# Two PSUM accumulators of a weight block: their matmuls alternate instead of following each other

## The chip, the cores and the metric

The kernel runs on one core of a Trainium2 chip. The metric is device time in microseconds, the median of several executions of the whole kernel on that core. A core has a matmul engine (TensorE; PE in the profile, its weight loads PEld), a vector engine (VectorE, DVE), a scalar engine (ScalarE, ACT), GpSimd (POOL) and DMA queues that SyncE (SP) and ScalarE issue here. [...]

## The reference

A decoder trunk of two layers on 256 tokens of width 2048, in fp32. Each layer projects the stream, mixes it, gates it, projects it back and normalizes it:

```python
def reference(x, mem, w_in, w_out, w_mem_kv, ln_g, ln_b, pool_w, pool_scale, w_kv_shared):
    h = x
    split_at = [BRANCH_WIDTH, 2 * BRANCH_WIDTH, 2 * BRANCH_WIDTH + MEM_WIDTH]
    for i in range(DEPTH):
        if i == N_A_LAYERS:
            k_blocks, v_blocks, k_mean = moba_shared_kv(h, w_kv_shared)
        u = h @ w_in[i]
        branch_in, gate_b, mem_q, gate_m = jnp.split(u, split_at, axis=-1)
        if i < N_A_LAYERS:
            branch = multiscale_pool(branch_in, pool_w[i], pool_scale[i])
        else:
            branch = moba_attention(branch_in, k_blocks, v_blocks, k_mean)
        mem_o = memory_attention(mem_q, mem, w_mem_kv[i])
        mixed = jnp.concatenate([branch * jax.nn.silu(gate_b), mem_o * jax.nn.silu(gate_m)], axis=-1)
        y = mixed @ w_out[i]
        h = layer_norm(DEEPNORM_ALPHA * h + y, ln_g[i], ln_b[i])
    return h
```

Layer 0 mixes by trailing means over 2, 4, 8 and 16 tokens and a small matrix per group, layer 1 by causal attention with 12 heads over the 256 tokens (one block, so no block selection is left). Both also attend to 256 memory tokens with 4 heads.

## The kernel before

Products are made exact enough by splitting: each fp32 operand becomes a rounded part (hi) and the exact rest (lo), both of type fp32r, and a product is hi·hi + hi·lo + lo·hi. The activations lie transposed as `xT`, `memT` and `zT` with the hi columns (256 tokens) beside the lo columns (256 tokens), 16 tiles along the contraction (k-tiles).

The weights stream through the kernel as a list of items, each one block of 128 x 1024. `run` (line 118) walks through the list: a block is loaded by SyncE 4 items ahead into one of 4 buffers `raw`, is split 3 items ahead (`LP`) by ScalarE (the rounded copy `wh`, line 68) and VectorE (the rest `wl`, line 69) into one of 4 buffers each, and is then consumed by TensorE. The code is written in the order in which each engine runs it; no scheduler moves anything (`manual_schedule`), and the semaphores between the engines follow from who reads what.

Two functions consume nearly all blocks.

- `proj_t` (line 152) makes 256 output channels, with the weights as the stationary operand. A block holds 4 k-tiles by 256 channels; two accumulators `acc[0]` and `acc[1]`, one PSUM bank each, take 128 channels each. For each k-tile and accumulator there are two matmuls: `wh` against the 512 hi and lo columns of the activations, and `wl` against the 256 hi columns. A block is 16 matmuls, four blocks make a projection. At the last k-tile (k = 15) the 256-column product comes first. There are 42 such projections: 168 blocks.
- `proj_n` (line 178) makes 512 output channels with the activations stationary. A block holds 2 k-tiles by 512 channels; accumulators `acc[0]` and `acc[1]` take 128 tokens each. For each k-tile and accumulator there are three matmuls of 512 columns: hi·`wh`, hi·`wl`, lo·`wh`. A block is 12 matmuls, eight blocks make a projection. There are 12 such projections: 96 blocks.

All blocks run through the matmul call at line 64. Inside a block, all matmuls of `acc[0]` stand before all of `acc[1]`; in the last block of a projection `done(0, acc[0])` stands behind the matmuls of `acc[0]`, `done(1, acc[1])` at the end. `done` is the reader of the accumulator: `fold` (lines 205 and 206: ScalarE copies the lo half, VectorE adds the hi half), or a split into values, or the addition to the residual with its statistics (lines 380 and 381). The accumulators rotate through four banks.

Between blocks stand the pieces of attention (`a`, `b`, `c` of the pairs, planned by `later` a given number of items ahead), the small pooling products (`pool_mix`, 256 columns each) and the transposes. At the end, `last` (line 705) multiplies the last output columns by weights that wait in the buffers of `xT` and `memT`.

Of the kernel before, what the change touches and what calls it, by code (L numbers as in the profile page):

```python
# [17 lines left out]
P = 128  # L18
T = 256                 # tokens (and memory tokens)
D = 2048  # L20
KT = D // P             # contraction tiles of a projection
HD = 128
# [9 lines left out]

BLK = 1024              # columns of a weight block: 4 k-tiles x 256 or 2 k-tiles x 512
RAW_BUFS = 4
W_BUFS = 4
LD = 4                  # blocks that loads run ahead
LEAD = 3                # first blocks, whose parts are read in turns
LD0 = 8                 # blocks that are loaded at once at the start
LP = 3                  # blocks that the splitting runs ahead


@with_exitstack
def trunk(ctx: ExitStack, tc: tile.TileContext, a: dict, out: bass.AP):
# [4 lines left out]

    # operands of products: [hi | lo] per tile, both exact in fp32r
    xT = sb.tile([P, KT, 2 * T], F32R, name="xT")  # L50
# [10 lines left out]

    # ---------------------------------------------------------------- basics
    def mm(o, l, r, start, stop):
        nc.tensor.matmul(o, l, r, start=start, stop=stop)  # L64

    def split(hi, lo, src):
        """hi = src rounded to fp32r, lo = the exact rest."""
        nc.scalar.activation(hi, src, AF.Copy)  # L68
        nc.vector.tensor_sub(lo, src, f(hi))  # L69

    # ---------------------------------------------------------------- stream
    items = []

    def collect(fn, *args):
        """The items that fn adds, taken out of the list."""
        base = len(items)
        fn(*args)
        got = items[base:]
        del items[base:]
        return got  # L80
# [5 lines left out]
    now = [0]  # L86
# [63 lines left out]

    # ---------------------------------------------------------------- projections
    def proj_t(mov, wblk, done):
        """256 output channels on partitions: done(n, psum[128, 512]) for n in 0, 1, where the
        products of hi and of lo tokens lie side by side."""
        acc = []

        def consume(kb):
            def go(wh, wl, k0=0, k1=4):
                if not acc:
                    acc.extend(ps.tile([P, 512], F32, name="acc", bufs=4) for _ in range(2))  # L160
                h = wh.rearrange("p (k n) -> p k n", n=256)
                l = wl.rearrange("p (k n) -> p k n", n=256)
                for n in range(2):
                    s = slice(n * P, (n + 1) * P)
                    for kk in range(k0, k1):
                        k = 4 * kb + kk
                        if k < KT - 1:
                            mm(acc[n], h[:, kk, s], mov[:, k], k == 0, False)
                        mm(acc[n][:, :T], l[:, kk, s], mov[:, k, :T], False, False)
                        if k == KT - 1:  # L170
                            mm(acc[n], h[:, kk, s], mov[:, k], False, True)
                    if kb == 3:
                        done(n, acc[n])
            return go
        for kb in range(4):
            item(wblk[kb], BLK, consume(kb))

    def proj_n(sta, wblk, done, korder=range(8), banks=("acc", "acc")):
        """512 output channels, tokens on partitions: done(t, psum[128, 512]) for t in 0, 1."""
        acc = []  # L180
        korder = list(korder)

        def consume(j, kb):
            def go(wh, wl):
                if j == 0:
                    acc.extend(ps.tile([P, 512], F32, name=b, bufs=4 if b == "acc" else 1) for b in banks)
                h = wh.rearrange("p (k n) -> p k n", n=512)
                l = wl.rearrange("p (k n) -> p k n", n=512)
                for t in range(2):
                    for kk in range(2):  # L190
                        k = 2 * kb + kk
                        xh = sta[:, k, t * P:(t + 1) * P]
                        xl = sta[:, k, T + t * P:T + (t + 1) * P]
                        first, last = j == 0 and kk == 0, j == 7 and kk == 1
                        mm(acc[t], xh, h[:, kk], first, False)
                        mm(acc[t], xh, l[:, kk], False, False)
                        mm(acc[t], xl, h[:, kk], False, last)
                    if j == 7:
                        done(t, acc[t])
            return go  # L200
# [16 lines left out]
    def to_gate(dst, base):  # L217
        """2 silu(x) = x (1 + tanh(x / 2))"""
        def done(n, acc):
# [19 lines left out]

    # ---------------------------------------------------------------- attention  # L240
    class Rows:
        """Row softmax in three steps: statistics, exponentials, division."""

# [20 lines left out]
    def gated(o, g, kt):  # L264
        """zT[kt] = o * silu(gate), of which g is the double"""
        zf = sb.tile([P, T], F32, name="zf", bufs=3)
# [49 lines left out]
    class MobaPair(Rows):  # L316
        """Two heads of causal attention over the own block: rows 0-127 see keys 0-127."""

# [31 lines left out]
        def c(self):  # L350
            v, g = self.st["v"], self.st["g"]
            o = ps.tile([P, 2, T], F32, name="o")
            for j in range(2):
                h = self.h0 + j
                # columns of ph: keys 0-127 of rows 0-255, then keys 128-255 of rows 128-255
                for m, (d, s) in enumerate(((o[:, j], slice(0, T)), (o[:, j, P:], slice(T, 384)))):
# [8 lines left out]
    def plan(pr, a, b, c):  # L365
        """Steps of a pair, by blocks from now: one engine's turn in each."""
        later(a, pr.a)
# [5 lines left out]

    # ---------------------------------------------------------------- residual and norm
    lnst = {}
# [33 lines left out]

    # ---------------------------------------------------------------- constants  # L410
    nc.vector.memset(eps_t[:, 0:1], EPS)
# [18 lines left out]

    # ---------------------------------------------------------------- memory branch
    st = {}

    def fresh(key, make):
        """st[key], as a tile that is allocated when its first part is written."""
        tiles = []
# [26 lines left out]
    def after(fn):  # L463
        """Attach fn to the item last added."""
        it = items[-1]
# [21 lines left out]

    # ================================================================ layer 0
    def load_act(t, src, kb):
        item(a[src][kb], BLK, None, ("act", t, kb))  # L490

    # memory keys and values side by side, while the activations arrive
    k0 = fresh("k", lambda: heads_tile("kk"))
# [17 lines left out]
    def pool_group(g):  # L511
        """Trailing means less the token, of the 384 channels in U, into zT as operands; as steps."""
        u = (U0, U1)[g % 2]
        src, d = u, 1
# [53 lines left out]
    def weave(main, extra):  # L568
        """An extra item after each of the first main ones."""
        for j, it in enumerate(main):  # L570
# [29 lines left out]

    # ================================================================ between the layers
    gbs = {}
# [6 lines left out]
    def h_transpose(kp):  # L609
        """Two k-tiles of the normed stream, transposed."""  # L610
        pt = ps.tile([P, 2, T], F32, name="pt" if kp % 2 else "o")
# [14 lines left out]

    # ================================================================ layer 1
    mem_q_gate(1)
# [18 lines left out]

    # the last columns of the output weights wait in the buffers of xT and memT
    def out_1():
        for n in range(3):  # L650
            proj_n(zT, [a["w_out"][1, n, kb] for kb in range(8)], to_residual(n), KORDER)

    # rows [g, g, g - g_hi, b, b - b_hi], the first of each rounded to fp32r: what the last
    # norm adds, (m0 - mean) / std * g + b, is one product of depth 5 with them
    gbt = {}
# [27 lines left out]

    # ================================================================ program
    items[0]["cuts"] = (0, T, 2 * T, BLK)
# [42 lines left out]

    # the last rows are centred by the mean of their first columns before all are known
    m0 = sb.tile([P, 2], F32, name="m0")  # L730
# [22 lines left out]

    # the last rows: (r - m0) g / std plus the product above, but for the first columns
    mv = sb.tile([P, 2], F32, name="mv", bufs=2)
# [28 lines left out]
def _cols_t(w):  # L784
    """[2048, N] -> [N/256, 4, 128, 4*256]: blocks of four k-tiles by 256 columns."""
    n = w.shape[1] // 256
# [3 lines left out]
def _cols_n(w):  # L790
    """[2048, N] -> [N/512, 8, 128, 2*512]: blocks of two k-tiles by 512 columns."""
    n = w.shape[1] // 512
# [3 lines left out]
def _act_t(x):  # L796
    """[256, 2048] -> [4, 128, 4*256]: transposed, blocks of four k-tiles."""
    return x.T.reshape(4, 4, P, T).transpose(0, 2, 1, 3).reshape(4, P, BLK)
# [37 lines left out]
```

## Time and profile before

| what | value |
|---|---|
| median of 3 runs | 829.24 us (828.7 to 829.42) |
| span of the profiled execution, first to last instruction | 826.7 us |
| own time of the profiled execution | not listed apart; the three runs lie 2.0 to 2.7 us above the span |
| TensorE busy | 813.9 us, 98% of the span |
| VectorE, ScalarE, GpSimd busy | 68%, 48%, 0% |
| matmuls, weight loads | 4436 each |
| mean granted TensorE clock | 0.997 |

How to read it: a row of the timeline is an instruction, or several equal ones in a row (x2), with its start and its duration. Matmuls are pipelined, so the duration of one (0.39 us for 512 columns) is longer than the distance to the start of the next; the distance of starts is what a matmul takes from the engine's time.

### The profile page before, as it was taken

How to read it: one execution, taken by the hardware profiler on the slowest of the kernel's cores; microseconds unless marked ns; L12 is line 12 of the kernel's file. 1: busy time of each engine (PE TensorE's matmuls, PEld its weight loads, DVE VectorE, ACT ScalarE, POOL GpSimd, SP SyncE). 2: the span in 40 equal slices, each digit the busy share in tenths (PEclk: the TensorE clock that was granted, in tenths of full speed). 3: DMA queues.
4: the chain of work that ended last, by engine and by line, in shares of the span. 5: the costliest groups of instructions: out<-in, count | busy, mean ns of one | idle time of the engine just before them, and what ended most of it. 6: DMA issues, size and time to landing. Idle time of an engine off the chain costs nothing.

```text
span 826.7 us, 11533 instructions
## 1 busy us (share of the span) xinstructions
PE 813.9 (98%) x4436; PEld 700.8 (85%) x4436; DVE 559.0 (68%) x793; ACT 397.3 (48%) x578; POOL 0.2 (0%) x4
## 2 busy tenths in 40 slices
PE   7999999999999999999999999999999999999995
PEld 6888888898888888888888888888888888888885
DVE  5686678667856555797667667576765667568746
ACT  6564555544545333545455445354554445545510
POOL 0000000000000000000000000000000000000000
PEclk9999999999999999999999999999999999999998
DMA  8876446457558655676554545546455554647742
GB/s 315 302 249 205 165 153 203 159 182 227 181 197 273 196 190 191 195 238 200 183 176 146 187 164 170 204 150 197 163 179 167 189 179 153 201 135 247 260 126 102
DMA packets 47163, 159.13 MB, mean 193 GB/s; under 512 B 5375, under 2 KB 7167, under 8 KB 46847
## 3 DMA queue, kind: packets, MB, share of 16 engines
q1 hardware_dynamic: 46080, 155.47, 56.9%
q10 hardware_dynamic: 1028, 2.93, 0.9%
q8 instruction: 34, 0.56, 0.3%
q14 instruction: 21, 0.17, 0.1%
HBM read 156.28 MB, written 2.10 MB: 192 GB/s over the span
## 4 chain that ended last, share of the span: by engine, by line
PE 98%; DVE 0%; DMA 0%; ACT 0%; DVEq 0%; issue 0%; SPq 0%
PE acc L64 89%; PE o L64 4%; PE s L64 2%; PE pt L64 2%; PE pt L347 0%; PE pt L297 0%; DMA raw<-in_w_mk 0%; PE o L615 0%; PE pt L615 0%; DVE res L779 0%; DVE res L760 0%; DVEq L832 0%; DVE stats L718 0%; DVE res L717 0%; ACT wh L68 0%
## 5 line engine op out<-in xcount | busy, mean ns | idle before, releaser
L69 DVE TENSOR_TENSOR wl<-raw,wh 128x1024 fp32r<-128x1024 f32 (+3 forms) x274 | 324.7, 1190 | 179.9 <-ACT wh L68 178.6
L64 PE MATMUL acc<-xT,wh 128*128 128x512 f32 x1216 | 422.0, 394 | 0.0
L68 ACT ACTIVATE wh<-raw 128x1024 fp32r<-128x1024 f32 (+3 forms) x274 | 281.4, 1031 | 220.2 <-PE acc L64 162.2
L64 PE MATMUL acc<-xT,wl 128*128 128x256 f32 x1216 | 327.9, 280 | 0.0
L64 PEld LDWEIGHTS acc<-xT,wh 128*128 128x128 f32 x1216 | 223.6, 188 | 43.5
L64 PEld LDWEIGHTS acc<-xT,wl 128*128 128x128 f32 x1216 | 228.5, 188 | 6.5 <-DVE wl L69 0.2
L64 PE MATMUL acc<-wh,zT 128*128 128x512 f32 x448 | 143.1, 397 | 0.0
L64 PEld LDWEIGHTS acc<-wh,zT 128*128 128x128 f32 x448 | 84.1, 188 | 19.9
L64 PE MATMUL acc<-wl,zT 128*128 128x512 f32 x224 | 88.0, 393 | 0.0
L64 PE MATMUL acc<-wh,xT 128*128 128x512 f32 x192 | 61.0, 396 | 0.0
L205 ACT ACTIVATE fold<-acc 128x256 f32<-128x256 f32 x72 | 27.7, 384 | 56.9 <-PE acc L64 55.8
L64 PE MATMUL acc<-memT,wh 128*128 128x512 f32 x128 | 46.8, 408 | 4.3 <-ACT wh L68 4.3
L64 PEld LDWEIGHTS acc<-wl,zT 128*128 128x128 f32 x224 | 42.1, 188 | 10.0
L64 PEld LDWEIGHTS acc<-wh,xT 128*128 128x128 f32 x192 | 36.0, 188 | 8.7
L64 PE MATMUL acc<-wl,xT 128*128 128x512 f32 x96 | 37.6, 392 | 0.0
L64 PE MATMUL acc<-memT,wl 128*128 128x256 f32 x128 | 35.5, 288 | 0.0
L206 DVE TENSOR_TENSOR fold<-acc,fold 128x256 f32<-128x256 f32 x72 | 29.5, 419 | 4.9 <-ACT fold L205 4.9
L64 PEld LDWEIGHTS acc<-memT,wh 128*128 128x128 f32 x128 | 24.7, 196 | 9.2 <-ACT wh L68 4.3
L68 ACT ACTIVATE zT<-zf 128x256 fp32r<-128x256 f32 x32 | 12.9, 415 | 39.7 <-DVE zf L267 35.4
L64 PEld LDWEIGHTS acc<-memT,wl 128*128 128x128 f32 x128 | 25.0, 196 | 1.0 <-DVE wl L69 0.2
L64 PEld LDWEIGHTS acc<-wl,xT 128*128 128x128 f32 x96 | 18.0, 188 | 4.3
L64 PE MATMUL acc<-xT,zT 128*128 128x256 f32 (+1 forms) x96 | 21.5, 318 | 0.0
(132 smaller groups left out, 617.9 us busy)
## 6 DMA issues: line engine op xcount, KB each, us to landing
raw<-in_w_in SPq DMA_DIRECT2D x128, 512.0 KB, 3.5
raw<-in_w_out SPq DMA_DIRECT2D x64, 512.0 KB, 4.3
raw<-in_w_sk SPq DMA_DIRECT2D x24, 512.0 KB, 4.2
raw<-in_w_sv SPq DMA_DIRECT2D x24, 512.0 KB, 3.5
raw<-in_w_mv SPq DMA_DIRECT2D x14, 512.0 KB, 5.4
raw<-in_w_mk SPq DMA_DIRECT2D x12, 512.0 KB, 4.4
raw<-in_xT SPq DMA_DIRECT2D x4, 512.0 KB, 5.2
res<-in_x ACTq DMA_DIRECT2D x2, 1024.0 KB, 5.7
```

The costliest lines, as they stand in the source:

```text
L64: nc.tensor.matmul(o, l, r, start=start, stop=stop)
L68: nc.scalar.activation(hi, src, AF.Copy)
L69: nc.vector.tensor_sub(lo, src, f(hi))
L205: nc.scalar.activation(dst, acc[:, T:], AF.Copy)
L206: nc.vector.tensor_add(dst, acc[:, :T], dst)
```

## The change

The loops inside a block are turned. In `proj_t`, for each k-tile the two `wh` products (of `acc[0]` and `acc[1]`, 512 columns each) now stand side by side, then the two `wl` products (256 columns each); at k = 15 the `wl` pair comes first. In `proj_n`, for each k-tile the three products are each done for `acc[0]` and at once for `acc[1]`. Both calls of `done` now stand behind all matmuls of the last block. The number and shapes of all matmuls and weight loads stay, and so do the order and number of instructions on ScalarE, VectorE, GpSimd and SyncE. Comments and docstrings are removed, too.

```diff
@@ proj_t
-                for n in range(2):
-                    s = slice(n * P, (n + 1) * P)
-                    for kk in range(k0, k1):
-                        k = 4 * kb + kk
-                        if k < KT - 1:
-                            mm(acc[n], h[:, kk, s], mov[:, k], k == 0, False)
-                        mm(acc[n][:, :T], l[:, kk, s], mov[:, k, :T], False, False)
-                        if k == KT - 1:
-                            mm(acc[n], h[:, kk, s], mov[:, k], False, True)
-                    if kb == 3:
+                for kk in range(k0, k1):
+                    k = 4 * kb + kk
+                    hi = [(acc[n], h[:, kk, n * P:(n + 1) * P], mov[:, k]) for n in range(2)]
+                    lo = [(acc[n][:, :T], l[:, kk, n * P:(n + 1) * P], mov[:, k, :T]) for n in range(2)]
+
+                    for o, wt, m in (hi + lo if k < KT - 1 else lo + hi):
+                        mm(o, wt, m, k == 0 and m.shape[-1] == 2 * T, k == KT - 1 and m.shape[-1] == 2 * T)
+                if kb == 3:
+                    for n in range(2):
                         done(n, acc[n])
@@ proj_n
-                for t in range(2):
-                    for kk in range(2):
-                        k = 2 * kb + kk
-                        xh = sta[:, k, t * P:(t + 1) * P]
-                        xl = sta[:, k, T + t * P:T + (t + 1) * P]
-                        first, last = j == 0 and kk == 0, j == 7 and kk == 1
-                        mm(acc[t], xh, h[:, kk], first, False)
-                        mm(acc[t], xh, l[:, kk], False, False)
-                        mm(acc[t], xl, h[:, kk], False, last)
-                    if j == 7:
+                for kk in range(2):
+                    k = 2 * kb + kk
+                    xh = [sta[:, k, t * P:(t + 1) * P] for t in range(2)]
+                    xl = [sta[:, k, T + t * P:T + (t + 1) * P] for t in range(2)]
+                    first, last = j == 0 and kk == 0, j == 7 and kk == 1
+                    for t in range(2):
+                        mm(acc[t], xh[t], h[:, kk], first, False)
+                    for t in range(2):
+                        mm(acc[t], xh[t], l[:, kk], False, False)
+                    for t in range(2):
+                        mm(acc[t], xl[t], h[:, kk], False, last)
+                if j == 7:
+                    for t in range(2):
                         done(t, acc[t])
```

On TensorE, in the last block of a `proj_t` projection of layer 1 (the accumulators are `acc_4253` and `acc_4254`, the block's split weights `wh_4247` and `wl_4248`), the end of one accumulator and the beginning of the other stood so before:

```order
L64 MATMUL acc_4253<-xT_63,wh_4247 128x512
L64 MATMUL acc_4253<-xT_63,wl_4248 128x256
L64 MATMUL acc_4253<-xT_63,wh_4247 128x512
L64 MATMUL acc_4253<-xT_63,wl_4248 128x256 x2
L64 MATMUL acc_4253<-xT_63,wh_4247 128x512
L64 MATMUL acc_4254<-xT_63,wh_4247 128x512
L64 MATMUL acc_4254<-xT_63,wl_4248 128x256
L64 MATMUL acc_4254<-xT_63,wh_4247 128x512
```

The 512- and 256-column products took turns, but for the last k-tile, where two of 256 and two of 512 columns meet. The end of the same block now:

```order
L64 MATMUL acc_4253<-xT_63,wh_4247 128x512
L64 MATMUL acc_4254<-xT_63,wh_4247 128x512
L64 MATMUL acc_4253<-xT_63,wl_4248 128x256
L64 MATMUL acc_4254<-xT_63,wl_4248 128x256
L64 MATMUL acc_4253<-xT_63,wl_4248 128x256
L64 MATMUL acc_4254<-xT_63,wl_4248 128x256
L64 MATMUL acc_4253<-xT_63,wh_4247 128x512
L64 MATMUL acc_4254<-xT_63,wh_4247 128x512
```

The banks take turns at every matmul, and the sizes now come in pairs: two of 512, two of 256; at the last k-tile four of 256 and then four of 512 with the next projection's first two.

In a `proj_n` block of the output projection of layer 1 (accumulators `acc_6654` and `acc_6655`), the first accumulator's part before was:

```order
L64 MATMUL acc_6654<-wh_6722,zT_65 128x512
L64 MATMUL acc_6654<-wl_6723,zT_65 128x512
L64 MATMUL acc_6654<-wh_6722,zT_65 128x512 x2
L64 MATMUL acc_6654<-wl_6723,zT_65 128x512
L64 MATMUL acc_6654<-wh_6722,zT_65 128x512
L64 MATMUL acc_6655<-wh_6722,zT_65 128x512
```

And now:

```order
L64 MATMUL acc_6654<-wh_6722,zT_65 128x512
L64 MATMUL acc_6655<-wh_6722,zT_65 128x512
L64 MATMUL acc_6654<-wl_6723,zT_65 128x512
L64 MATMUL acc_6655<-wl_6723,zT_65 128x512
L64 MATMUL acc_6654<-wh_6722,zT_65 128x512
L64 MATMUL acc_6655<-wh_6722,zT_65 128x512
```

All have 512 columns before and after; what moves is the bank, and that the same activations are no longer stationary twice in a row.

## Rows read from the trace of the kernel before

**Rows 1.** The page: busy time by engine, and the granted clock in 40 slices.

```profile
PE 813.9 (98%) x4436; PEld 700.8 (85%) x4436; DVE 559.0 (68%) x793; ACT 397.3 (48%) x578; POOL 0.2 (0%) x4
...
PEclk9999999999999999999999999999999999999998
```

**Rows 2.** The page, groups by line: busy us, mean ns | idle before.

```profile
L64 PE MATMUL acc<-xT,wh 128*128 128x512 f32 x1216 | 422.0, 394 | 0.0
...
L205 ACT ACTIVATE fold<-acc 128x256 f32<-128x256 f32 x72 | 27.7, 384 | 56.9 <-PE acc L64 55.8
```

**Rows 3.** Timeline of TensorE, an inner `proj_t` block: start us, duration us.

```profile
464.23 0.39 PE L64 MATMUL acc<-xT,wh 128*128 128x512 f32 x1
...
465.50 0.28 PE L64 MATMUL acc<-xT,wl 128*128 128x256 f32 x1
465.62 0.39 PE L64 MATMUL acc<-xT,wh 128*128 128x512 f32 x1
465.85 0.28 PE L64 MATMUL acc<-xT,wl 128*128 128x256 f32 x1
```

**Rows 4.** Timeline of TensorE: block starts among four `proj_t` projections of layer 0.

```profile
125.63 0.40 PE L64 MATMUL acc<-xT,wh 128*128 128x512 f32 x1
...
128.41 0.39 PE L64 MATMUL acc<-xT,wh 128*128 128x512 f32 x1
...
133.96 0.39 PE L64 MATMUL acc<-xT,wh 128*128 128x512 f32 x1
...
139.53 0.39 PE L64 MATMUL acc<-xT,wh 128*128 128x512 f32 x1
...
145.07 0.39 PE L64 MATMUL acc<-xT,wh 128*128 128x512 f32 x1
...
170.08 0.40 PE L64 MATMUL acc<-xT,wh 128*128 128x512 f32 x1
```

**Rows 5.** Timeline of TensorE: the end of a `proj_t` projection, the next one's beginning.

```profile
471.87 0.39 PE L64 MATMUL acc<-xT,wh 128*128 128x512 f32 x1
472.09 0.40 PE L64 MATMUL acc<-xT,wl 128*128 128x256 f32 x2
472.33 0.63 PE L64 MATMUL acc<-xT,wh 128*128 128x512 f32 x2
472.80 0.28 PE L64 MATMUL acc<-xT,wl 128*128 128x256 f32 x1
```

**Rows 6.** Timeline of TensorE: the first of 18 pooling products, and what follows them.

```profile
172.87 0.40 PE L64 MATMUL pt<-zT,wh 128*128 128x256 f32 x2
...
174.98 0.39 PE L64 MATMUL acc<-xT,wh 128*128 128x512 f32 x1
```

**Rows 7.** Timeline of TensorE, `proj_n`: two rows with 12 matmuls from start to start.

```profile
743.69 0.63 PE L64 MATMUL acc<-wh,zT 128*128 128x512 f32 x2
...
746.49 0.63 PE L64 MATMUL acc<-wh,zT 128*128 128x512 f32 x2
```

**Rows 8.** Timeline of TensorE, in `last`: two rows with 3 matmuls from start to start.

```profile
797.31 0.39 PE L64 MATMUL acc<-memT,zT 128*128 128x512 f32 x1
...
797.99 0.39 PE L64 MATMUL acc<-memT,zT 128*128 128x512 f32 x1
```

**Rows 9.** Timeline of TensorE: the first and the third matmul of the kernel.

```profile
4.28 0.79 PE L64 MATMUL acc<-memT,wh 128*128 128x512 f32 x1 [4.28 <-ACT wh L68]
...
5.12 0.63 PE L64 MATMUL acc<-memT,wh 128*128 128x512 f32 x1
```

**Rows 10.** Timelines of ScalarE, VectorE and TensorE around 54 us.

```profile
51.43 0.60 ACT L68 ACTIVATE vv<-o 128x512 fp32r<-128x512 f32 x1 [0.80 <-PE o L64]
...
53.00 1.22 DVE L69 TENSOR_TENSOR wl<-raw,wh 128x1024 fp32r<-128x1024 f32 x1 [0.26 <-ACT wh L68]
...
54.01 0.40 PE L64 MATMUL acc<-xT,wh 128*128 128x512 f32 x1
54.28 0.39 PE L64 MATMUL acc<-xT,wl 128*128 128x256 f32 x1
```

## The prediction

> **What bounds the kernel now.** I read the page's busy times first, then the groups by line, then TensorE's timeline. TensorE is busy for 813.9 of 826.7 us, at the full granted clock in all slices but the last [rows 1], and the largest group of matmuls has no idle time before it [rows 2]. The other engines are at 68% and less. So the time is the sum of what the 4436 matmuls take one behind the other. A change that only reorders them can act in three ways: it changes the distance from one matmul's start to the next one's, it moves a wait onto TensorE, or it takes one away. The timeline gives the distances. In an inner block of `proj_t`, 512 and 256 columns alternate with 0.23 and 0.12 us, and the eight matmuls of the first accumulator take 1.39 us (464.23 to 465.62) [rows 3]. In `proj_n`, 12 matmuls of 512 columns take 2.80 us, 0.2333 each [rows 7].
>
> **Does a bank that changes make a matmul cheaper?** The trace of before already has such changes, one in the middle of every block and one at its end. At 465.50 the last matmul of one bank starts and at 465.62 the first of the other; the distance, 0.12, and the next, 0.23, are those of the pairs before [rows 3]. Over all of the trace's starts, the 193 changes of this kind (a 256-column product on `xT`, then a 512-column one on another bank) have a mean distance of 118.0 ns, and the 912 that stay in the bank 117.4. I therefore cost the new bank at 0. Both ends: the reading of one row is good to 0.01 us, the two means differ by +0.6 ns; with 1 ns either way and 3840 matmuls (168 blocks of 16, 96 of 12) the term lies between -3.8 and +3.8 us. From 0.43 ns per matmul on it would decide by itself.
>
> **Does the new order of sizes cost something?** This is the term that moves the sum. In `proj_t` the change does more than alternate banks: 512, 256, 512, 256 becomes 512, 512, 256, 256. Before, equal sizes meet only at k = 15, once per accumulator. Four projections of layer 0 run from 125.63 to 170.08 without anything between them, 44.45 us for 16 blocks. Their inner blocks take 5.55 us a pair (128.41 to 133.96) or 5.54 (139.53 to 145.07), 2.7725 each [rows 4]; 16 of these would be 44.36. The other 0.09 us belong to the eight places where two of 256 and two of 512 meet: about 10 ns a place. Rows 5 show one: two of 256 from 472.09 to 472.33, two of 512 from 472.33 to 472.80, 0.71 us, where two alternating pairs take 2.7725/4 = 0.693.
>
> What a place costs when every four matmuls are one is not in the trace, so I bound it. The low end: only the two neighbours of equal size cost what they cost in streams of one size, 0.2333 [rows 7] and, for 18 pooling products of 256 columns, 2.11/18 = 0.1172 [rows 6]; the other two distances stay those of the alternation. Two equal neighbours then take 0.3505 where a pair takes 0.3466, so +4 ns per four. If all four cost what the streams do, it is 2 x 4 = +8 ns. The isolated place, 10 ns, is the high end, with up to 17 by the single row pair above (0.710 - 0.693). I take +8: it lies beside the row with the same operands and tiles (10), and part of those 10 may be the price of falling out of step and back, which a regular pattern doesn't pay each time. There are 42 projections x 16 k-tiles = 672 fours: 672 x 8 ns = +5.4 us. The 84 places that exist already (42 x 2) are dissolved into them: 84 x 10 ns = -0.8 us. `proj_n` has 512 columns before and after, and its distances are the same whether the stationary activations repeat or not as far as a whole block shows it (2.80 us for blocks in which a third of the steps repeat them) [rows 7]: 0, with +-0.5 us for 1152 matmuls at 0.4 ns.
>
> [...]
>
> **What moves on the other engines.** Their instruction order is unchanged, but `done(0)` waits for the end of the block instead of its middle, 1.39 us later [rows 3]. Queued behind the waiting `fold` on ScalarE (0.384 us [rows 2]) is the split of the weight block four items ahead. That costs nothing where the splitting is three blocks ahead, 3 x 2.77 = 8.3 us; without this cover each of the 54 projections could lose that 0.384 us, 21 us in all, but a shift that is absorbed once is not paid again.
>
> The cover is thin at one place. Around 54 us the values' second split on ScalarE starts at 51.43 and takes 0.60; behind it comes the rounding of the next weight block, whose rest VectorE makes from 53.00 to 54.22, and TensorE's second matmul there starts 0.27 behind its first instead of 0.23, the next pair is late as well; the block loses 0.16 us [rows 10]. In the new kernel both splits stand behind the end of the block, so the chain moves by about 0.5 us, while the `wl` operand is wanted 0.23 us later, behind two products of 512. I take +0.2 us (between -0.16 and +0.5).
>
> At the start the opposite happens. The first matmul of the kernel shows 0.79 us, the third, of the same shape, 0.63 [rows 9]: the 0.16 us between them are the second one's wait for `wl`, which VectorE hasn't finished. With two 512-column products in front, `wl` is wanted later by a whole one of them, and the wait goes: -0.2 us (between -0.25 and 0). The two cancel.
>
> **Sum.** 5.4 - 0.8 + 0 = +4.6 us. The span of the profiled execution becomes 826.7 + 4.6 = 831.3; the median of the runs is 2.5 us above that span, and that difference stays: 833.8 us, 0.55% slower.
>
> **Rivals.**
> 1. No change: the fours settle into a step of their own that costs what the alternation costs, or at most the 4 ns of the low end. For it: a matmul of 512 columns takes 0.22 us at one place (471.87 to 472.09) and 0.235 at the next [rows 5]; such distances compensate each other in part, and the average is what counts. Against it: 84 places that all cost something. At 0 ns per four it gives -0.8, 828.4 us; at 4 ns, 2.7 - 0.8 = +1.9, 831.1 us. [...]
> 2. Faster: streams of equal size can run quicker than the alternation. In `last`, 3 matmuls of 512 columns take 0.68 us, 0.2267 each [rows 8], and with 0.1172 for 256 columns a pair would be 0.3439 instead of 0.3466; two pairs in each of 672 fours give -3.6, with the 84 places -4.4 us: 824.8 us. The same sign has a bank turnaround that shows only when every matmul changes its bank: 1 ns is 3.8 us. Against the first: there the moving operand is `xT` or `memT` and the weights are `zT`; where `wh` is stationary and `xT` moves, 512 behind 512 takes 0.235 [rows 5]. With the 84 places gone it decides from 1.2 ns per four on. Against the second are rows 3.
> 3. Much slower: the late `done(0)` makes TensorE wait in each projection. It would take 0.2 us per projection, 54 of them, 11 us: 840 us. Against it stands the cover of three blocks; it would have to eat 8.3 us first.
>
> **How the numbers follow.** A kernel like this tells 0.2% (1.66 us) from no change. The forecast (6 to 14 ns per four, +3.2 to +8.6 us) has 0.58; rival 1 (0 to 6 ns) 0.27, of which 0.03 lie above 3.7 ns, where the bound of 0.2% is crossed; rival 2 0.11, rival 3 0.04. Slower than 830.9: 0.58 + 0.04 + 0.03 = 0.65. Within 0.2%: 0.24. Faster than 827.6: 0.11. The range runs from the lower bound of no change, 827.6, to 12 ns per four with the small terms at their high ends (8.1 - 0.8 + 0.5 = 7.8): 837.0. Outside are rival 2, rival 3 and the top of the forecast, some 0.18. The forecast's own range is 832.4 to 837.8.
>
> **What would show it.** In the new timeline an inner `proj_t` block takes 4 x 8 = 32 ns more than 2.77 us, 2.80 to 2.81; the first and last blocks no longer differ from it much; two of 512 columns take about 0.465 and two of 256 about 0.235. `proj_n` blocks stay at 2.80. TensorE's list of waits has nothing new of over 0.5 us. The prediction is wrong if inner `proj_t` blocks stay at 2.77 or fall below, if `proj_n` blocks leave 2.80 (then the bank or the repeated stationary operand matters), or if waits of TensorE on ScalarE or VectorE appear at ends of projections.

## The result, and the profile after

The kernel after takes 835.18 us (median of 4 runs, 834.62 to 835.64), the kernel before in the same comparison 828.97 us (4 runs, 828.63 to 829.42). The ratio is 1.0074, with a 95% interval of 1.0059 to 1.0088: 0.7% slower. The forecast was 833.8 us. The profiled execution of after has a span of 833.3 us and an own time of 835.62.

From the page of after, the span, the busy times and the largest group of matmuls:

```profile
span 833.3 us, 11533 instructions
...
PE 820.1 (98%) x4436; PEld 702.9 (84%) x4436; DVE 560.6 (67%) x793; ACT 392.6 (47%) x578; POOL 0.2 (0%) x4
...
L64 PE MATMUL acc<-xT,wh 128*128 128x512 f32 x1216 | 379.9, 397 | 0.0
```

Beside [rows 1, 2]: TensorE's busy time grew from 813.9 to 820.1 us with the same 4436 matmuls, nearly the whole 6.6 us of the span, and the large group still has no idle time before it (0.0, the last number of its row). So matmuls became dearer; TensorE did not begin to wait. Its list of waits says the same (engine, line and tile waited for, total us, times, longest):

```profile
PE acc L64 <- ACT wh L68: 4.7, 1, 4.7
PE pt L769 <- DVE cc L766: 2.8, 1, 2.8
PE acc L64 <- ACT cct L771: 0.4, 1, 0.4
```

These three places wait in before too, with 4.3, 2.8 and 0.4 us. The first is the arrival of the first weight block. Five experiments below begin with the same two matmuls as after (banks only, the two with runs of eight, and after with 32 and with 1696 bytes more) and show 4.2 to 4.4 there, so I don't put these 0.4 us down to the change.

Next, TensorE's timeline (start, duration, operation, count): an inner block of `proj_t` in layer 0, from its first two matmuls to those of the next block.

```profile
130.04 0.63 PE L64 MATMUL acc<-xT,wh 128*128 128x512 f32 x2
130.51 0.40 PE L64 MATMUL acc<-xT,wl 128*128 128x256 f32 x2
130.75 0.63 PE L64 MATMUL acc<-xT,wh 128*128 128x512 f32 x2
131.22 0.40 PE L64 MATMUL acc<-xT,wl 128*128 128x256 f32 x2
...
132.87 0.39 PE L64 MATMUL acc<-xT,wh 128*128 128x512 f32 x1
```

The block takes 2.83 us where [rows 4] had 2.7725. A four (two of 512, two of 256) takes 0.71. Over the trace inner blocks come in two lengths, 2.813 and 2.827 us, which is 10.0 and 13.5 ns more per four than before. The distances between neighbours in the inner blocks tell which matmul pays: a 256 that follows a 512 begins 235.5 ns behind it, against 229.2 in the alternation, and a 512 that follows a 512 begins after 232.4, while a matmul behind a 256 begins after 117.4 to 119.1 ns, against 117.5. It is mostly the 512-column products that got dearer, the second of a pair most.

In `proj_n` (here in layer 1) six matmuls take 1.40 us:

```profile
776.27 0.63 PE L64 MATMUL acc<-wl,zT 128*128 128x512 f32 x2
776.74 1.09 PE L64 MATMUL acc<-wh,zT 128*128 128x512 f32 x4
777.67 0.63 PE L64 MATMUL acc<-wl,zT 128*128 128x512 f32 x2
```

That is 0.2333 each, as in [rows 7]. Summed over all distances of starts, `proj_t` on `xT` went from 424.6 to 430.2 us, `proj_t` on `memT` from 47.0 to 47.5, `proj_n` on `zT` from 157.1 to 157.1. With the 0.4 us of the first wait, these are 6.5 of the 6.6 us.

### The profile page after: what moved, and what is told of

It is laid out like the page before. It is cut to its first block, busy times and chain, and to the rows that moved or that the text cites. A ratio compares the mean times of both kernels' runs of the same rounds, so it can differ in the third digit from the quotient of the medians.

```text
span 833.3 us, 11533 instructions
## 1 busy us (share of the span) xinstructions
PE 820.1 (98%) x4436; PEld 702.9 (84%) x4436; DVE 560.6 (67%) x793; ACT 392.6 (47%) x578; POOL 0.2 (0%) x4
## 4 chain that ended last, share of the span: by engine, by line
PE 98%; DVE 0%; DMA 0%; ACT 0%; DVEq 0%; issue 0%; SPq 0%
PE acc L64 89%; PE o L64 3%; PE s L64 2%; PE pt L64 2%; PE pt L349 0%; PE pt L299 0%; DMA raw<-in_w_mk 0%; PE o L617 0%; PE pt L617 0%; DVE res L781 0%; DVE res L762 0%; DVEq L834 0%; DVE stats L720 0%; DVE res L719 0%; ACT wh L68 0%
## 5 line engine op out<-in xcount | busy, mean ns | idle before, releaser
L64 PE MATMUL acc<-xT,wh 128*128 128x512 f32 x1216 | 379.9, 397 | 0.0
L64 PEld LDWEIGHTS acc<-xT,wl 128*128 128x128 f32 x1216 | 223.0, 188 | 52.0 <-DVE wl L69 0.5
L64 PE MATMUL acc<-xT,wl 128*128 128x256 f32 x1216 | 237.0, 281 | 0.0
L64 PEld LDWEIGHTS acc<-xT,wh 128*128 128x128 f32 x1216 | 189.0, 189 | 2.9
L64 PE MATMUL acc<-wh,zT 128*128 128x512 f32 x448 | 124.3, 395 | 0.0
L64 PE MATMUL acc<-wl,zT 128*128 128x512 f32 x224 | 70.6, 396 | 0.0
L64 PE MATMUL acc<-wh,xT 128*128 128x512 f32 x192 | 52.9, 394 | 0.0
L64 PEld LDWEIGHTS acc<-wl,zT 128*128 128x128 f32 x224 | 42.0, 188 | 10.1
L64 PE MATMUL acc<-memT,wh 128*128 128x512 f32 x128 | 41.9, 412 | 4.7 <-ACT wh L68 4.7
L64 PE MATMUL acc<-wl,xT 128*128 128x512 f32 x96 | 30.3, 396 | 0.0
L64 PE MATMUL acc<-memT,wl 128*128 128x256 f32 x128 | 25.6, 287 | 0.0
```

## The experiments

Each is a few lines on the kernel before or after and was timed beside the kernel before on the same chip. The first three take the change apart.

**Banks only.** In `proj_t` the sizes keep alternating, and the bank changes at every second matmul (0, 1, 1, 0), where before changes it twice in a block of 16; both `done` stand at the end.

```diff
+                for kk in range(k0, k1):
+                    k = 4 * kb + kk
+                    for fn, n in (((hi, 0), (hi, 1), (lo, 0), (lo, 1)) if k == 0 else
+                                  ((lo, 0), (hi, 0), (lo, 1), (hi, 1)) if k == KT - 1 else
+                                  ((hi, 0), (lo, 1), (hi, 1), (lo, 0))):
+                        fn(n, kk)
+                if kb == 3:
+                    for n in range(2):
                         done(n, acc[n])
```

> proj_t alone is changed: the banks alternate at nearly every matmul, and the sizes keep alternating too (512 on bank 0, 256 on bank 1, 512 on bank 1, 256 on bank 0). Theory S (the order of sizes costs, the bank nothing): inner proj_t blocks stay at 2.77 us, and the time is that of the kernel before, 829 us, or 0.4 us less because only one place per projection is left where equal sizes meet. Theory B (a bank that changes at each matmul is what costs): blocks of 2.81 us or more, 834 to 835 us.

Measured: 829.25 us, ratio 1.000 [0.999, 1.001]. The banks change at every second matmul here, not at nearly every one as the expectation has it.

**Sizes only**: each accumulator's matmuls stay together, and the sizes come in pairs over two k-tiles.

```diff
+                    for p0 in range(k0, k1, 2):
+                        ks = range(p0, min(p0 + 2, k1))
+                        hi = [(acc[n], h[:, kk, s], mov[:, 4 * kb + kk], kb + kk == 0, 4 * kb + kk == KT - 1) for kk in ks]
+                        lo = [(acc[n][:, :T], l[:, kk, s], mov[:, 4 * kb + kk, :T], False, False) for kk in ks]
+                        for args in (lo + hi if 4 * kb + p0 + 2 == KT else hi + lo):
+                            mm(*args)
```

> proj_t alone is changed: each accumulator's matmuls stay together as in the kernel before, but the sizes come in pairs inside it (512 of two k-tiles, then 256 of the same two). Theory S: inner proj_t blocks of 2.81 to 2.83 us and 834.5 to 836 us although no bank alternates. Theory B: 2.77 us and 829 us.

Measured: 834.9 us, ratio 1.0071 [1.0056, 1.0086]. The timeline of TensorE in the first of the two, from a block's beginning to the next one's:

```profile
129.47 0.39 PE L64 MATMUL acc<-xT,wh 128*128 128x512 f32 x1
129.70 0.28 PE L64 MATMUL acc<-xT,wl 128*128 128x256 f32 x1
...
132.25 0.39 PE L64 MATMUL acc<-xT,wh 128*128 128x512 f32 x1
```

and in the second:

```profile
129.59 0.63 PE L64 MATMUL acc<-xT,wh 128*128 128x512 f32 x2
130.06 0.40 PE L64 MATMUL acc<-xT,wl 128*128 128x256 f32 x2
130.29 0.63 PE L64 MATMUL acc<-xT,wh 128*128 128x512 f32 x2
...
132.41 0.63 PE L64 MATMUL acc<-xT,wh 128*128 128x512 f32 x2
```

With alternating sizes the block takes 2.78 us by these rounded starts and 2.773 in most inner blocks, as before. With pairs in one and the same bank it takes 2.82 (2.813 in most). A bank that changes at every second matmul costs nothing that shows; the order of sizes alone costs, within the noise, what the whole change costs. A small part may still belong to both together: the length of 2.827 us, which 22 inner blocks of after have, doesn't appear here, and `proj_t` on `xT` takes 429.4 us in all against 430.2; the medians, 834.9 and 835.18, don't tell the two kernels apart. The late `done(0)` costs nothing either, since the first of these kernels has it.

**`proj_n` only** (the new loop of `proj_n` from the diff, `proj_t` as before):

> Only proj_n has the new order, proj_t that of the kernel before. Theory S and the trace of the changed kernel: proj_n blocks of 2.80 us as before, 829 us. Theory B: the 1152 matmuls of proj_n pay for the bank as well, by 2.5 ns each as in proj_t, +2.9 us, 832 us.

Measured: 829.19 us, ratio 1.0003 [0.9994, 1.0012], 2.80 us per block. This half of the change is free, and here the bank does change at every matmul. It doesn't tell why 512 columns take 0.2333 here and 0.2267 in `last` [rows 7, 8]. The next runs ask whether where the operands lie in SBUF sets that pace.

**Weights moved by 32 bytes.** The activations `xT`, `memT` and `zT` are allocated first, the weight buffers `raw`, `wh` and `wl` behind `stats`. A tile of 32 bytes per partition that nobody uses moves the weights, and with them the smaller tiles that are allocated later; the first run does it to before, the second to after.

```diff
     stats = sb.tile([P, 2, 5, 6], F32, name="stats")
+    pad = sb.tile([P, 8], F32, name="pad")
```

> The kernel before with 32 more bytes per partition ahead of the weight buffers, so that raw, wh and wl begin at multiples of 64 bytes instead of 32 beyond one; xT, memT and zT stay where they are, at multiples of 64. Theory A (what a matmul takes beyond its columns depends on where its operands begin): proj_n falls from 233.3 to the 226.7 ns that last shows, whose operands all begin at multiples of 64, so 2.72 us a block, 1152 x 6.7 = -7.7 us, 821 us. Theory N (the start doesn't matter): 829 us and 2.80 us.

> The changed kernel with the 32 bytes ahead of the weight buffers of the run e4_line_shift, where proj_t blocks with alternating sizes took 2.805 us instead of 2.773 and proj_n blocks 2.79. Theory S1 (pairs of equal sizes cost some 10 ns per four whatever the placement): 4 x 10 ns more on each of 168 blocks, 833.0 + 6 = 839 us. Theory S2 (the cost is a matter of how the order and the placement fall together): proj_t blocks at or below the 2.805 of e4, 831 to 834 us.

Measured: before with the tile 832.99 us, ratio 1.0046 [1.0031, 1.0061]; after with the tile 832.0, 1.0026 [1.0015, 1.0037]. Neither theory of the first run held: neither is the time the same nor is it shorter. A tile without a reader costs 3.7 us. TensorE's timeline in before with the tile, a block of `proj_t`:

```profile
129.57 0.39 PE L65 MATMUL acc<-xT,wh 128*128 128x512 f32 x1
...
132.38 0.40 PE L65 MATMUL acc<-xT,wh 128*128 128x512 f32 x1
```

and in after with the tile:

```profile
129.18 0.62 PE L65 MATMUL acc<-xT,wh 128*128 128x512 f32 x2
129.65 0.40 PE L65 MATMUL acc<-xT,wl 128*128 128x256 f32 x2
...
131.97 0.39 PE L65 MATMUL acc<-xT,wh 128*128 128x512 f32 x1
```

With the weights 32 bytes further, the alternation takes 2.81 us a block and the pairs 2.79. The order that loses 6.2 us in the original placement wins 1.0 us in this one by the medians. The intervals of the two ratios overlap, so the traces are the better witness: `proj_t` takes 1.9 us less in all with the pairs. So the cost that I had looked for in the order belongs to the order and the placement together.

**Runs of eight**, in the original placement: per block eight products of 512 columns, then eight of 256 (in the last block the other way round).

```diff
+                for args in (lo + hi if kb == 3 else hi + lo):
+                    mm(*args)
```

> proj_t alone is changed: in a block, the eight 512-column products stand first and then the eight of 256 columns (reversed in the last block of a projection), banks in turns. Theory P (each pass from the alternation into a pair of equal sizes costs 10 ns): fewer passes, a block costs 2 x 10 ns at most over 2.773, 829 to 831 us. Theory R (a row of 512-column products has its own, slower step, 233 ns against 229 in the alternation, and a row of 256 the 117 of the pooling products): 8 x 0.2333 + 8 x 0.1172 = 2.804 us a block, 829.2 + 168 x 0.031 - 0.8 = 833.6 us.

Measured: 834.15 us, ratio 1.0062 [1.0045, 1.0079]. One block on TensorE's timeline:

```profile
129.48 2.04 PE L64 MATMUL acc<-xT,wh 128*128 128x512 f32 x8
131.35 1.10 PE L64 MATMUL acc<-xT,wl 128*128 128x256 f32 x8
132.29 0.86 PE L64 MATMUL acc<-xT,wh 128*128 128x512 f32 x3
```

Eight of 512 take 1.87 us, 0.2337 each, eight of 256 0.94, 0.1175 each; the block takes 2.81. Here each size runs at the pace of its stream, that of [rows 6, 7], and the alternation is quicker than the streams are. The pairs are no quicker than streams either.

**Everything moved, and both moved.** 32 bytes ahead of `xT` move all tiles alike; 32 ahead of `xT` and 32 ahead of the weights move all and leave 32 bytes more between the operands.

```diff
+    pad0 = sb.tile([P, 8], F32, name="pad0")
     xT = sb.tile([P, KT, 2 * T], F32R, name="xT")
```

> The kernel before with 32 more bytes per partition ahead of xT: xT, memT and zT now begin 32 bytes beyond a multiple of 64 and raw, wh and wl at a multiple; their distance is that of the kernel before. Theory D (only the distance of the operands in memory counts): 829 us and blocks of 2.77 and 2.80. Theory A2 (each operand's own start counts): blocks leave these values, as in e4, by up to 0.04 us; no side is favoured.

> The kernel before with 32 more bytes ahead of xT and 32 ahead of the weight buffers: all of them begin 32 bytes beyond a multiple of 64, and their distance is that of e4. Theory D: as e4, 833 us, proj_t blocks of 2.805. Theory A2: other values than both.

Measured: 829.3 us, 1.0003 [0.9994, 1.0013], and 833.0, 1.0046 [1.0031, 1.0061]. All moved alike, a block of `proj_t` still takes 2.77 us:

```profile
128.60 0.39 PE L65 MATMUL acc<-xT,wh 128*128 128x512 f32 x1
...
131.37 0.39 PE L65 MATMUL acc<-xT,wh 128*128 128x512 f32 x1
```

So for these 32 bytes it is not where an operand lies that counts, but how far the weights lie from the activations.

**Other distances.** The traces hold no addresses. By my count of the tiles' sizes in the order of the kernel, each taken as rounded up to a multiple of 32 bytes, which is an assumption, the weight buffers of before begin 2400 bytes past a multiple of 4096 from the beginnings of `xT`, `memT` and `zT`. A tile of 424 words (1696 bytes) in the place of `pad` makes the distance a multiple of 4096 by this count; it was run with before's order and with after's. A tile of 16 words (64 bytes) leaves the distance's remainder by 64 as it was.

> The kernel before with 1696 more bytes per partition ahead of the weight buffers, so that wh and wl lie a multiple of 4096 bytes from xT, memT and zT, as the operands of last do among each other. Theory L (the distance modulo more than 64 bytes counts; last's 226.7 and 120.0 ns belong to this distance): proj_n blocks fall to 12 x 226.7 = 2.72 us, proj_t blocks stay at 8 x (226.7 + 120.0) = 2.773 without the extra at k = 15, 829.2 - 7.7 - 0.8 = 821 us. Theory M (only the distance modulo 64 counts): as in e4_line_shift, 833 us.

> The changed kernel with the same 1696 bytes. Theory L: the order of sizes costs nothing at this distance, proj_t blocks 2.773 and proj_n blocks 2.72 us as in e10, 821 us. Theory M: as e5_after_shifted, 832 us.

> The kernel before with 64 more bytes ahead of the weight buffers: the distance modulo 64 stays 32 as before, the distance modulo 128 changes. Theory M: 829 us, blocks of 2.773 and 2.800. Theory L: the blocks leave these values in either direction.

Measured: before's order + 1696 bytes 829.22 us, 0.9996 [0.9987, 1.0006]; after's order + 1696 bytes 825.26, 0.9946 [0.9929, 0.9964]; before's order + 64 bytes 834.21, 1.0052 [1.0034, 1.0071]. The unchanged total of the first hides two large terms. From its timeline, a `proj_t` block and a `proj_n` block:

```profile
129.46 0.40 PE L65 MATMUL acc<-xT,wh 128*128 128x512 f32 x1
...
132.28 0.40 PE L65 MATMUL acc<-xT,wh 128*128 128x512 f32 x1
...
284.85 0.39 PE L65 MATMUL acc<-wl,zT 128*128 128x512 f32 x1
...
287.57 0.39 PE L65 MATMUL acc<-wl,zT 128*128 128x512 f32 x1
```

`proj_n` takes 2.72 us a block, 0.2267 per matmul: the pace that `last` has [rows 8], where both operands lie in `xT`, `memT` and `zT`, by the same count a multiple of 4096 bytes apart. Over the trace `proj_n` gains 7.0 us, and the alternating `proj_t` (2.82 here by the rounded starts, 2.830 in most inner blocks) loses 6.6.

Not all blocks go along. Eight inner blocks of this run, all near the attention's small products of layer 1, take 2.773 or 2.779 us, two of them here one behind the other:

```profile
489.62 0.40 PE L65 MATMUL acc<-xT,wh 128*128 128x512 f32 x1
...
492.39 0.40 PE L65 MATMUL acc<-xT,wh 128*128 128x512 f32 x1
...
495.17 0.40 PE L65 MATMUL acc<-xT,wh 128*128 128x512 f32 x1
```

Their order, buffers and distance are those of the blocks of 2.830, so these don't settle the pace alone; what ran just before differs.

With after's order the loss is smaller, 2.79 us a block:

```profile
128.72 0.62 PE L65 MATMUL acc<-xT,wh 128*128 128x512 f32 x2
129.19 0.40 PE L65 MATMUL acc<-xT,wl 128*128 128x256 f32 x2
...
131.51 0.40 PE L65 MATMUL acc<-xT,wh 128*128 128x512 f32 x1
```

That version beats both kernels. In its list of waits a new one appears:

```profile
PE acc L65 <- DVE wl L70: 1.2, 2, 1.0
```

The longer of the two stands at 775 us, in the output projection of layer 1, where the faster `proj_n` now outruns the splitting of the weights. At 64 bytes both kinds of block are slower than before:

```profile
130.31 0.39 PE L65 MATMUL acc<-xT,wh 128*128 128x512 f32 x1
...
133.11 0.39 PE L65 MATMUL acc<-xT,wh 128*128 128x512 f32 x1
...
288.59 0.40 PE L65 MATMUL acc<-wl,zT 128*128 128x512 f32 x1
...
291.41 0.39 PE L65 MATMUL acc<-wl,zT 128*128 128x512 f32 x1
```

2.80 and 2.82 us. The distance by 64 alone doesn't decide, then: before has by this count the same remainder and takes 2.77 and 2.80.

**Runs of eight at a multiple of 4096** by that count (the order of `e6` above with the 1696 bytes):

> The proj_t order of e6_runs_of_8 (eight products of 512 columns, then eight of 256) with the 1696 bytes of e10_same_offset; proj_n in the order of the kernel before. If streams of one size take at this distance what last and proj_n of e10 show (226.7 and 120.0 ns), a proj_t block falls from the 2.787 us of e11 to 8 x 0.2267 + 8 x 0.1200 = 2.773, 168 x 14 ns = -2.3 us against e11's 825.3: 823 us. If the weights' changing place inside a block (1024 bytes per k-tile) matters as well, the block stays between 2.79 and 2.83 us, 825.5 to 832 us.

Measured: 824.32 us, 0.9941 [0.9924, 0.9958]. Inner blocks take 2.793 us, first ones 2.766, last ones 2.801: the expectation held for the first blocks alone. The interval lies on that of the pairs at this distance, so the two orders can't be told apart by time. It is the fastest of all kernels run here, by as little.

A table of what each order of sizes takes in an inner block of `proj_t`, and `proj_n` in its blocks (most frequent lengths, us), by bytes put between the operands; "-" wasn't run:

| order | 0 | 32 | 64 | 1696 |
|---|---|---|---|---|
| alternating | 2.773 | 2.806, 2.814 | 2.800 | 2.830 (eight: 2.773, 2.779) |
| pairs, two banks | 2.813, 2.827 | 2.787 | - | 2.787 |
| runs of eight | 2.807 to 2.81 | - | - | 2.793 |
| `proj_n` (512 only) | 2.800 | 2.78 to 2.80 | 2.805 to 2.815 | 2.720 |

## Why the prediction was right, and where it wasn't

- **The bank, 0: right.** It rested on two rows at a change of bank and on two means (118.0 and 117.4 ns). Banks alone moved the time by nothing that can be measured, 1.000 [0.999, 1.001]; there they change at every second matmul. In `proj_n` they change at every one, 1.0003 and 2.80 us a block, so the bank turnaround of rival 2 doesn't show either.
- **The order of sizes, +5.4 us: the right cause, undersized.** Sizes alone gave 1.0071, the whole change 1.0074. From the sums of distances, `proj_t` grew by 5.6 + 0.5 us; less the 0.14 us at 54 us (below) and plus the 0.84 us of the old places that dissolved, that is 6.8 us over 672 fours, 10.1 ns each, not 8. The step that failed is the choice inside the bounds: "part of those 10 may be the price of falling out of step and back, which a regular pattern doesn't pay each time". The regular pattern pays it each time, 10 or 13.5 ns in inner blocks. The row of the isolated place was the better measure than the reasoning that discounted it. The 2.1 ns too few are 1.4 us, which is what the forecast lacked. Rival 1 (0 to 6 ns) fell with these 10 ns. What the prediction doesn't have is the placement: it took the price for a matter of the neighbours' sizes, and at 1696 bytes the same neighbours save time. The isolated places show that as well: with 1696 bytes a last block and the first one behind it, which hold two such places, take 2.829 + 2.817 us where two inner ones take 2 x 2.830, so 7 ns less a place.
- **The +8 as such was nearly the number of something else.** It was made from the pace of streams, and the runs of eight show that: (2.81 - 2.773)/4 is 9 ns, 834.15 us.
- **`proj_n`, 0: right** (ratio 1.0003 alone, 2.80 us in the trace).
- **The late `done(0)`, hidden: right.** The waits list has nothing new, and rival 3 (840 us) fell with it.
- **Around 54 us, +0.2: the sign fits, the size isn't shown.** The timeline of TensorE in after:

```profile
54.45 0.40 PE L64 MATMUL acc<-xT,wl 128*128 128x256 f32 x2
54.69 0.63 PE L64 MATMUL acc<-xT,wh 128*128 128x512 f32 x2
55.36 0.50 PE L64 MATMUL acc<-xT,wl 128*128 128x256 f32 x2
55.70 0.63 PE L64 MATMUL acc<-xT,wh 128*128 128x512 f32 x2
```

  From 54.69 to 55.70 the four takes 1.01 us instead of 0.71. The block loses 0.30 us where before lost 0.16 [rows 10], so +0.14. But this place differs from run to run. The run with `proj_n` only, whose `proj_t` is that of before, loses 0.43 us here, and 0.54 us pass between the starts of two matmuls that are 0.23 apart elsewhere:

```profile
54.23 0.40 PE L64 MATMUL acc<-xT,wh 128*128 128x512 f32 x1
54.77 0.39 PE L64 MATMUL acc<-xT,wl 128*128 128x256 f32 x1
```

  The other runs with before's order lose 0.10 to 0.17 us, the three with after's 0.30 to 0.51, banks only 0.49, and sizes only and the runs of eight at most 0.01. A difference of 0.14 between two traces is inside that spread.
- **At the start, -0.2: wrong.** The timeline of after begins so:

```profile
4.70 1.22 PE L64 MATMUL acc<-memT,wh 128*128 128x512 f32 x2 [4.70 <-ACT wh L68]
5.72 0.63 PE L64 MATMUL acc<-memT,wl 128*128 128x256 f32 x2
6.15 1.05 PE L64 MATMUL acc<-memT,wh 128*128 128x512 f32 x2
```

  The first two of 512 take 1.02 us from start to start where two take 0.86 a little later. The 0.16 us are still there with `wl` far from being needed: they belong to the first matmul, not to a wait of the second. I had read a long duration [rows 9] as a neighbour's wait. The starts of the weight loads fit this: the first load begins together with its matmul, at 4.70, the second 0.165 us later, and the second matmul 0.430 us after that, against 0.42 from the third load to the third matmul. That third load begins together with the second matmul, at 5.29; the first load has no matmul ahead of it. In before the weight load of `wl` does wait for VectorE, until 4.74, but the second matmul begins 0.59 us after the first in both kernels.
- **Rival 2, streams of equal size at 0.2267: a true pace under another condition.** I had excluded it because the operands differ, and said no more on what in them mattered. Of what differs, the distance between the operands alone is enough: with 1696 bytes more between them `proj_n` has exactly this pace, 2.72 us for 12. In the original placement no block of `proj_t` or `proj_n` shows it. Its sign was right elsewhere: with 32 and 1696 bytes between the operands the pairs are quicker than the alternation.

The pace of matmuls depends here on how far apart their two operands lie: a `proj_n` block that is otherwise the same takes 2.72 to 2.82 us. What stays open: why the distance moves the pace, what other distances would do (only 0, 32, 64 and 1696 bytes were put between), why the alternation is the quickest order at one distance and the slowest at another, and why blocks with the same order and distance come in two lengths. Traffic of the other engines and of DMA is not what sets the pace. In before the `proj_n` matmuls on `zT` and `xT` beside which neither ScalarE nor VectorE works (13 of them) and those beside which no DMA packet is under way (58) begin 233.2 ns apart, the others 233.4; with 1696 bytes these are 226.7 (7), 227.3 (49) and 226.9.

## What to carry to other kernels

When TensorE is busy for 98% of the span, a reordering is costed by distances from start to start, and an odd place in the trace that already has the new neighbours is a better price than a reasoned discount on it, as long as the placement stays. A new order of matmuls should be compared at more than one placement of its operands before it is kept or dropped: here the sign of the result changed with 1696 unused bytes, and by the traces with 32. A total that doesn't move is worth taking apart by stage, since terms of 7.0 and 6.6 us can cancel in it.

## What was not expected of the hardware

- An unused tile of 32 bytes per partition between activations and weights costs 3.7 us of 829 (ratio 1.0046), one of 64 bytes 4.8 us (1.0052), and the same 32 bytes ahead of both nothing (1.0003).
- With 1696 bytes more between weights and activations, by my count a multiple of 4096 from each other, 512 fp32r columns take 0.2267 us in `proj_n` instead of 0.2333, and with the products in pairs or in eights the kernel takes 825.26 or 824.32 us, 0.5 to 0.6% less than before.
- The alternation of 512 and 256 columns takes 693 ns per two pairs in the original placement, less than the two streams at their own pace (2 x 0.2337 + 2 x 0.1175 = 702).
- At one distance (1696 bytes more) the alternation has two lengths, 2.830 us a block in most and 2.773 or 2.779 in eight that stand near attention products.
